# Seven-product FFN input projection: weight pieces split in an order of their own

## The chip, the cores and the metric

One core of a Trainium2 chip runs the whole program. The metric is device time in microseconds (us) of one execution; smaller is better. A profile is one execution taken by the hardware profiler.

## What is computed

One layer of a decoder trunk on 512 tokens of width 1024: a mixer with three branches, and then a gated FFN, each between two norms. The change lies in the FFN. Cut to that, the reference is

```python
h2 = rms_norm(x, g_pre_ffn) * (1 + scale2) + shift2
gt, up = jnp.split(h2 @ w_ffn_in, 2, axis=-1)       # w_ffn_in: 1024 x 5632
f = (jax.nn.silu(gt) * up) @ w_ffn_out              # w_ffn_out: 2816 x 1024
x = x + (gate2 * rms_norm(f, g_post_ffn))
```

All of it is in float32. The kernel gets this precision from matrix products on reduced operands: each operand is split into a high part (a cast, on ScalarE) and a low part (the operand less its high part, on VectorE), and a product is made of three matmuls, high by high, high by low and low by high.

## The kernel before

The hidden width of 2816 is 22 row blocks of 128. Two row blocks make a **unit**, so there are 11 units (u = 0 to 10), each with its gate and its up columns. Within a unit the product h2 by w_ffn_in is seen as a 2 x 2 block product: the weights in two row blocks by two halves of the 1024 inputs, the tokens in two halves of 256. Eight block products would be needed; the kernel forms seven (numbered 1 to 7) from sums of weight blocks and sums of token blocks. For each product q of unit u there is one **piece** of weights, 128 x 1024, and `split` (L153) makes its high part `whi` on ScalarE (L154) and its low part `wlo` on VectorE (L155). Four buffers hold the high and four the low parts, so four pieces can be alive.

What a piece is split from is said in `wino_piece` (L274). Pieces 1, 2, 4 and 7 come from the raw weights `wraw` (7 after a VectorE sum into them, L284, made when piece 4 is split). Pieces 5, 6 and 3 come from one tile `wsum` in turn: VectorE forms it for piece 5 (L282); when piece 5 is split, GpSimd issues a transfer that adds a block of raw weights into the tile, for piece 6 (L291); when piece 6 is split, another one for piece 3. For units 0 and 1 the first sums are made by transfers too (`wino_open`, L261). There are two `wsum` tiles and four raw tiles, loaded by SyncE's queue (L253).

`step` (L1159) makes one product: it fetches its piece, runs `flush()`, and issues 24 matmuls (L1171). Products 1, 2, 3 and 5 multiply token tiles in `hbh`/`hbl`; 4, 6 and 7 multiply the token sums `tx`. Two products add into a bank that another has begun: product 2 into that of 1, product 3 into that of 5. Between them the gate work is done: `gated_m1` (L1192) makes three VectorE operations, called c here, after product 7 (L1195, which reads 7; L1196, which reads the bank of product 5; L1198, which reads 4), then three ScalarE operations `sg` (L164 to L166), and leaves two VectorE products for the next `flush`. `gated_m0` (L1184) and `third_of` (L1201) do the like for the other quarters.

The order of the work in this stage is the order of the code, engine by engine: a manual schedule holds for TensorE, VectorE and ScalarE. Two things set it. The products of a unit from 2 on run in the order 5, 1, 4, 6, 7, 2, 3 (loop from L1302); units 0 and 1 run together, amid the steps of the norm that makes the last tokens' h2. And `piece()` (L226) decides when a piece is split: the list `WINO` (L239) names the pieces in the order in which they are used, and each `step` first splits, in the order of that list, up to `at["look"]` pieces ahead (4 in this stage, 3 for a while, 3 elsewhere). So the split of the piece three products on stands in the queues of ScalarE and VectorE ahead of what follows this product there.

After the last unit the second FFN product follows. Its operand `f4s[u]` is split into `fparts` by `f_split` (L1330), and its first rows also take in a modulation row made from `mod_w` on the side (`mods_in_turn`, L961, whose matmuls are `pmr`).

Of the kernel before, what the change touches and what calls it, by code (L numbers as in the profile page):

```python
# [8 lines left out]
FR = mybir.dt.float32r  # L9
# [4 lines left out]
P = 128  # L14
# [18 lines left out]
def hybrid_block(ctx: ExitStack, tc, x, c, mod_w, mod_b, g_pre_mix, g_post_mix, g_pre_ffn,  # L33
# [29 lines left out]
    hl = gp.tile([P, KD, T], FR, tag="h_lo", name="hl")  # L63


    tqs = ExitStack()
    tq = tqs.enter_context(tc.tile_pool(name="tq", bufs=1, side="right"))

    def q2(name, dt=F32):
        return tq.tile([P, 512], dt, tag="q2", name=name, bufs=12)  # L70
# [82 lines left out]
    def split(hi, lo, src):  # L153
        act.copy(hi, src)  # L154
        vec.tensor_tensor(lo, src, hi.bitcast(F32), ALU.subtract)  # L155
# [12 lines left out]


    chunks, pieces, raws = [], [], []  # L170
    at = {"dma": 0, "split": 0, "use": 0, "raw": 0, "look": LOOK}

    def w_cols(src, c0, n=256):

# [27 lines left out]
    def split_piece():  # L202
# [20 lines left out]
        pieces[at["split"]] = (hi, lo)  # L223
        at["split"] += 1

    def piece():  # L226

        i = at["use"]
        at["use"] += 1
        while at["split"] < min(i + at["look"], n_pieces):  # L230
            with tc.high_priority() if at["split"] < 5 else nullcontext():
                split_piece()
        return pieces[i]


# [1 line left out]

    NU = MF // 2
    WINO = [(u, q) for q in (1, 2, 5, 6, 7, 4, 3) for u in range(2)]  # L239
    WINO += [(u, q) for u in range(2, NU) for q in (5, 1, 4, 6, 7, 2, 3)]  # L240
    units = {}
    late_pool = {}

# [875 lines left out]
    for tp2 in range(2):  # L1119
        tbs = (2 * tp2, 2 * tp2 + 1)  # L1120
        pos = {tb: [bank("pwo") for _ in range(2)] for tb in tbs}
        ws = {}
        if tp2:
            at["look"] = 4
        for k in range(KD - LATE):
            ws[k] = piece()
            for tb in tbs:
                wo_mm(pos[tb], tb, ws[k], k)
            if todo and k >= 2:
                h2_tiles(todo.pop(0))  # L1130
# [25 lines left out]
        while later:  # L1156
            later.pop(0)()

    def step(q, o, start, stop):  # L1159

        hi, lo = piece()
        flush()
        for g in range(2):
            cs = slice(g * 256, g * 256 + 256)
            for k in range(4):
                if q in tb_of:
                    xh, xl = hbh[:, tb_of[q], k, :], hbl[:, tb_of[q], k, :]
                else:
                    xh, xl = (t_[k // 2][:, k % 2, :] for t_ in tx[q])
                for part, (a_, b_) in enumerate(((hi, xh), (hi, xl), (lo, xh))):  # L1170
                    pe.matmul(o[:, cs], a_[:, g, k, :], b_,  # L1171
                              start=(start and g + k + part == 0),
                              stop=(stop and k == 3 and part == 2), skip_group_check=True)
# [29 lines left out]
        vec.tensor_tensor(u2, p5, u2, ALU.add)  # L1203
        gated_m0(f4, u2, 1)

    def f_parts(u, parts_):
        split(parts_[0], parts_[1], f4s[u])
        fhs.append(parts_[0])
        fls.append(parts_[1])
    f4s, fhs, fls, pts = [], [], [], {}  # L1210
    rest = ctx.enter_context(ExitStack())
    rest.enter_context(tc.manual_schedule(engines={ET.PE, ET.DVE, ET.Activation}))
    if True:
        late_mm(2)
        chain_sq(2, pos[2])
        chain_norm(2, pos[2])
        late_mm(3)
        chain_x1(2, pos[2], lambda: t2("sq2"))
        chain_sq(3, pos[3])
        chain_norm2(2)  # L1220
        chain_norm(3, pos[3])
        chain_h2(2)
        ma.close()
        fp = ctx.enter_context(tc.tile_pool(name="fp", bufs=1, reuse_waits="tile"))
        fxs = ExitStack()
        fx = fxs.enter_context(tc.tile_pool(name="fx", bufs=1, reuse_waits="tile"))
        late_pool.update(fp=fp, fx=fx)
        wino_open()
        pb_ = {1: [], 5: [], 6: [], 7: [], 4: []}

        def fresh(q):
            pb_[q].append(bank(f"pf{q}"))
            step(q, pb_[q][-1], True, True)
        u2s = [temp("u2", 512, 2) for _ in range(2)]
        fresh(1)
        act.copy(u2s[0], pb_[1][0])
        chain_x1(3, pos[3], lambda: temp("sg1", 512))
        fresh(1)
        act.copy(u2s[1], pb_[1][1])
        chain_norm2(3)  # L1240
        step(2, pb_[1][0], False, True)
        pts[0] = h2_tr(2)

        t1_, b22, t2_, t3_, t4_ = (f4_tile(n) for n in ("t1r", "b22", "t2r", "t3r", "t4r"))

        def k4(t_, u):
            return t_[:, u, :].rearrange("p (k t) -> p k t", k=4)

        def tx_tiles(q):
            tx[q] = [[q2("tx", FR).rearrange("p (k t) -> p k t", k=2) for _ in range(2)]  # L1250
                     for _ in range(2)]

        def parts_of(q, t_, u):
            for k0 in (0, 2):
                ts = slice(u * P, (u + 1) * P)
                h_, l_ = (t__[k0 // 2][:, :, ts] for t__ in tx[q])
                split(h_, l_, k4(t_, u)[:, k0:k0 + 2, :])
        tks = [slice(u * P, (u + 1) * P) for u in range(2)]
        def t1_of(u):
            vec.tensor_tensor(k4(t1_, u), raws2[0, u], pts[u][0], ALU.subtract)  # L1260
            split(hbh[:, 3, :, tks[u]], hbl[:, 3, :, tks[u]], k4(t1_, u))
            act.copy(k4(b22, u), pts[u][1])
        t1_of(0)
        chain_h2(3)
        at["look"] = 3
        step(2, pb_[1][1], False, True)
        at["look"] = 4
        pts[1] = h2_tr(3)
        t1_of(1)
        tx_tiles(6)  # L1270
        for u in range(2):
            vec.scalar_tensor_tensor(k4(t2_, u), k4(t1_, u), -1.0, k4(b22, u), op0=ALU.mult,
                                     op1=ALU.subtract)
            parts_of(6, t2_, u)
        for u in range(2):
            f4s.append(f4_tile("f4"))
            gated_m0(f4s[u], pb_[1][u], 0)
            flush()
        fresh(5)
        fresh(5)  # L1280
        tx_tiles(7)
        for u in range(2):
            vec.tensor_tensor(k4(t3_, u), k4(b22, u), pts[u][0], ALU.subtract)
            parts_of(7, t3_, u)
        for u in range(2):
            fresh(6)
            vec.tensor_tensor(u2s[u], pb_[6][u], u2s[u], ALU.add)
        for u in range(2):
            vec.tensor_tensor(k4(t4_, u), raws2[1, u], k4(t2_, u), ALU.add)
        tx_tiles(4)  # L1290
        for u in range(2):
            parts_of(4, t4_, u)
            split(hbh[:, 2, :, tks[u]], hbl[:, 2, :, tks[u]], k4(b22, u))
        fresh(7)
        fresh(7)
        for u in range(2):
            fresh(4)
            gated_m1(f4s[u], pb_[4][u], pb_[5][u], pb_[7][u], u2s[u])
        for u in range(2):
            step(3, pb_[5][u], False, True)  # L1300
            third_of(f4s[u], pb_[5][u], u2s[u])
        for u in range(2, NU):  # L1302
            f4s.append(f4_tile("f4"))
            p5 = bank("pf5")
            step(5, p5, True, True)
            if u == NU - 1:
                t_ = fp.tile([P, 2, 2, T], FR, tag="raw4", name="fparts", bufs=1)
                f_parts(0, (t_[:, 0], t_[:, 1]))
            p1, u2 = bank("pf1"), temp("u2", 512, 2)
            step(1, p1, True, True)  # L1310
            act.copy(u2, p1)
            p4 = bank("pf4")
            step(4, p4, True, True)
            p6 = bank("pf6")
            step(6, p6, True, True)
            vec.tensor_tensor(u2, p6, u2, ALU.add)  # L1316
            p7 = bank("pf7")
            step(7, p7, True, True)
            gated_m1(f4s[u], p4, p5, p7, u2)
            step(2, p1, False, True)  # L1320
            gated_m0(f4s[u], p1, 0)
            step(3, p5, False, True)
            third_of(f4s[u], p5, u2)
        flush()
    at["look"] = LOOK
    fxs.close()
    tqs.close()
    fo = ctx.enter_context(tc.tile_pool(name="fo", bufs=1, reuse_waits="tile"))

    def f_split(u):  # L1330

        f_parts(u, [fo.tile([P, 2, T], FR, tag="f4o", name="fparts", bufs=10) if u < 6
                    else f4_tile("fparts", FR) for _ in range(2)])
    f_split(1)

    def mah_late():
        t_ = wp.tile([P, 1024], FR, tag="whi", name="mah")
# [7 lines left out]

    def fo_mm(o, tb, w, k0, cs):
        for k in range(2):
            mm3(o[:, cs], fhs[k0 // 2][:, k, blk(tb)], fls[k0 // 2][:, k, blk(tb)],
                w[0][:, k, cs], w[1][:, k, cs], k0 + k == 0, k0 + k == MF - 1)

    NPF = MF // 2
# [77 lines left out]
```

## Time and profile before

| what | value |
|---|---|
| runs, median (lowest to highest of 3) | 883.24 us (882.63 to 884.37) |
| the profiled execution's own time | 881.74 us |
| its span, first to last instruction | 880.0 us |
| granted TensorE clock, mean of the span | 0.958 |
| TensorE busy | 778.7 us (88%) |
| VectorE busy | 561.9 us (64%) |
| ScalarE busy | 423.1 us (48%) |
| GpSimd busy | 149.5 us (17%) |
| stage of the seven products, first to last of its matmuls | 424.4 to 741.4 us |

In profile lines, PE is TensorE, DVE VectorE, ACT ScalarE, POOL GpSimd and SP SyncE. A line of a timeline gives start and duration in us, the engine, the line of the program, the operation, "out<-in" by the program's tile names, the shape, and in brackets how long the engine had been idle before it and what released it. A granted clock of 1.0 is full speed. Busy time of TensorE counts a matmul to its modelled end, and neighbours overlap, so the distance between starts is the better measure.

### The profile page before, as it was taken

The numbers are of one execution on the slowest core, as the hardware profiler recorded it, in microseconds if no ns is written. First come the engines' busy times: TensorE is split into PE (matmuls) and PEld (weight loads), VectorE is DVE, ScalarE is ACT, GpSimd is POOL, SyncE is SP. The second block draws the span as 40 slices with busy tenths as digits, with TensorE's granted clock in tenths as the row PEclk, the third lists the DMA queues.
The fourth block names the chain that finished last, engine by engine and source line by source line (L and its number), as shares of the span: only waits on it lengthen the run. The fifth ranks groups of instructions, "written<-read, shape, count | busy, mean of one in ns | idle before, by whom it ended". The sixth has DMA issues, their size and how long they took to land. (4 is left out here: it accounts for less than half of the span.)

```text
span 880.0 us, 11357 instructions
## 1 busy us (share of the span) xinstructions
PE 778.7 (88%) x4357; PEld 670.8 (76%) x4357; DVE 561.9 (64%) x812; ACT 423.1 (48%) x707; POOL 149.5 (17%) x193
## 2 busy tenths in 40 slices
PE   4899999999999999999778777887779778889997
PEld 3779887767788888878668776887779777768886
DVE  5999776688465665469568654666555656772224
ACT  5558445757663736247455434444334445442212
POOL 4354323346201020110120101010110101000000
PEclk9999999999999999999969988988889899999999
DMA  9963422124166877485759167535664336452302
GB/s 280 291 198 96 144 70 74 48 95 146 58 206 180 263 189 253 99 304 148 188 99 239 32 137 144 110 61 118 144 129 97 80 79 180 155 171 104 108 0 96
DMA packets 122597, 123.51 MB, mean 140 GB/s; under 512 B 4076, under 2 KB 95264, under 8 KB 122544
## 3 DMA queue, kind: packets, MB, share of 16 engines
q1 hardware_dynamic: 111120, 100.67, 37.4%
q0 software_dynamic: 10656, 21.06, 13.9%
q10 hardware_dynamic: 768, 1.07, 0.3%
q8 instruction: 34, 0.56, 0.3%
q14 instruction: 19, 0.16, 0.1%
HBM read 103.38 MB, written 2.10 MB: 120 GB/s over the span
## 5 line engine op out<-in xcount | busy, mean ns | idle before, releaser
L155 DVE TENSOR_TENSOR wlo<-wraw,whi 128x1024 fp32r<-128x1024 f32 (+1 forms) x133 | 162.8, 1234 | 115.0 <-ACT whi L154 114.4
L154 ACT CAST whi<-wraw 128x1024 fp32r<-128x1024 f32 (+1 forms) x133 | 136.6, 1032 | 133.6 <-PE pgt L159 32.6
L1171 PE MATMUL pf<-hbh,whi 128*128 128x256 f32 x352 | 109.8, 312 | 62.5 <-DVE c L1196 53.2
L1171 PEld LDWEIGHTS pf<-hbh,whi 128*128 128x128 f32 x352 | 76.0, 216 | 65.3 <-issue 55.3
L1171 PE MATMUL pf<-hbl,whi 128*128 128x256 f32 x352 | 107.5, 305 | 0.1
L1171 PE MATMUL pf<-hbh,wlo 128*128 128x256 f32 x352 | 106.9, 304 | 0.0
L1171 PE MATMUL pf<-tx,whi 128*128 128x256 f32 x528 | 95.5, 282 | 2.0 <-ACT whi L154 1.0
L155 DVE TENSOR_TENSOR wlo<-wsum,whi 128x1024 fp32r<-128x1024 f32 x33 | 40.2, 1224 | 81.7 <-ACT whi L154 81.7
L1171 PEld LDWEIGHTS pf<-tx,whi 128*128 128x128 f32 x528 | 81.1, 188 | 2.6 <-ACT whi L154 1.2
L1171 PE MATMUL pf<-tx,wlo 128*128 128x256 f32 x264 | 75.3, 285 | 2.8 <-DVE wlo L155 2.7
L1171 PEld LDWEIGHTS pf<-hbl,whi 128*128 128x128 f32 x352 | 76.1, 216 | 0.5 <-DVE hbl L155 0.4
L158 PE MATMUL pgt<-hh,whi 128*128 128x512 f32 x192 | 75.7, 394 | 0.0
L1171 PEld LDWEIGHTS pf<-hbh,wlo 128*128 128x128 f32 x352 | 75.5, 215 | 0.0
L160 PE MATMUL pgt<-hh,wlo 128*128 128x512 f32 x192 | 75.4, 393 | 0.0
L159 PE MATMUL pgt<-hl,whi 128*128 128x512 f32 x192 | 75.0, 390 | 0.0
L154 ACT CAST whi<-wsum 128x1024 fp32r<-128x1024 f32 x33 | 34.2, 1041 | 78.3 <-DMA wsum<-wraw 53.5
L291 POOL DMA_DIRECT2D wsum<-wraw x22 | 26.0, 1182 | 261.1 <-DVE wlo L155 246.6
L158 PE MATMUL pfo<-whi,fparts 128*128 128x512 f32 x154 | 61.4, 399 | 2.5 <-ACT fparts L154 2.5
L160 PE MATMUL pfo<-whi,fparts 128*128 128x512 f32 x154 | 61.7, 401 | 0.5 <-DVE fparts L155 0.5
L159 PE MATMUL pfo<-wlo,fparts 128*128 128x512 f32 x154 | 61.3, 398 | 0.0
L1171 PEld LDWEIGHTS pf<-tx,wlo 128*128 128x128 f32 x264 | 49.7, 188 | 4.5 <-DVE wlo L155 4.4
L991 DVE SCALAR_TENSOR_TENSOR macc<-wraw,sc,macc 128x512 f32<-128x512 f32 x56 | 42.9, 766 | 10.0 <-ACT macc L989 5.5
(389 smaller groups left out, 1688.7 us busy)
## 6 DMA issues: line engine op xcount, KB each, us to landing
wraw<-in_w_ffn_in_dram SPq DMA_DIRECT2D x44, 512.0 KB, 6.6
wraw<-in_w_in_dram SPq DMA_DIRECT2D x20, 1024.0 KB, 5.2
wraw<-in_mod_w_dram SPq DMA_DIRECT2D x16, 1024.0 KB, 5.9
wsum<-wraw POOLq DMA_DIRECT2D x24, 512.0 KB, 6.1
wraw<-in_w_ffn_out_dram SPq DMA_DIRECT2D x10, 1024.0 KB, 5.4
wraw<-in_mod_w_dram SPq DMA_DIRECT2D x16, 512.0 KB, 6.2
wraw<-in_w_o_dram SPq DMA_DIRECT2D x8, 1024.0 KB, 5.8
gate<-gate POOLq DMA_DIRECT2D x14, 256.0 KB, 4.0
```

The source lines that it names most:

```text
L154: act.copy(hi, src)
L155: vec.tensor_tensor(lo, src, hi.bitcast(F32), ALU.subtract)
L158: pe.matmul(o, whi, xhi, start=start, stop=False)
L159: pe.matmul(o, whi, xlo, start=False, stop=False)
L160: pe.matmul(o, wlo, xhi, start=False, stop=stop)
L291: nc.gpsimd.dma_start(un["s"], un[0][q - 5], accum_op=ALU.add)
L991: vec.scalar_tensor_tensor(acc, mw[:, r], c_, acc, op0=ALU.mult, op1=ALU.add)
L1171: pe.matmul(o[:, cs], a_[:, g, k, :], b_, start=(start and g + k + part == 0), stop=(stop and k == 3 and part == 2), skip_group_check=True)
```

## The change

Five things are edited.

1. The list `WINO` no longer follows the products' order. From unit 3 on, the piece of product 3 of the unit before comes third, behind pieces 5 and 1; the last unit's own piece 3 comes last. `step` now gets the unit and looks its piece up by (unit, product), so the products keep their order.
2. The first `step` calls get a smaller look-ahead each (3, 3, 2, 1, then an explicit `split_to(wino0 + 5)`, then 2 and 3), and the output projection's second half looks 3 pieces ahead where it looked 4.
3. In units 0 and 1, the token sums of product 7 are made before the first gate products, and these stand ahead of the first product 6.
4. The hidden parts of unit 1 are split in the last unit, ahead of its product 3, where they were split after all units.
5. The hidden parts of units 1 to 3 are split in halves into tiles of the pool `tq`, which is no longer closed; the pool `fo` has 4 buffers where it had 10.

```diff
+    def split_to(n):
+        while at["split"] < min(n, n_pieces):
...
+                split_piece()
...
     WINO = [(u, q) for q in (1, 2, 5, 6, 7, 4, 3) for u in range(2)]
-    WINO += [(u, q) for u in range(2, NU) for q in (5, 1, 4, 6, 7, 2, 3)]
+
+    for u in range(2, NU):
+        WINO += [(u, 5), (u, 1)] + [(u - 1, 3)] * (u > 2) + [(u, q) for q in (4, 6, 7, 2)]
+    WINO.append((NU - 1, 3))
...
-        if tp2:
-            at["look"] = 4
...
-    def step(q, o, start, stop):
-
-        hi, lo = piece()
+    wino0 = at["use"]
+
+    def step(u, q, o, start, stop, ahead=4):
+
+        i = at["use"]
+        at["use"] += 1
+        split_to(i + ahead)
+        hi, lo = pieces[wino0 + WINO.index((u, q))]
         flush()
...
+        if u < 4:
+            for parts_ in (fhs, fls):
+                parts_.append([q2("fparts", FR) for _ in range(2)])
+            for m in range(2):
+                split(fhs[u][m], fls[u][m], f4s[u][:, m, :])
...
-        fresh(1)
+        fresh(1, 3)
         act.copy(u2s[0], pb_[1][0])
         chain_x1(3, pos[3], lambda: temp("sg1", 512))
-        fresh(1)
+        fresh(1, 3)
         act.copy(u2s[1], pb_[1][1])
         chain_norm2(3)
-        step(2, pb_[1][0], False, True)
+        step(0, 2, pb_[1][0], False, True, 2)
...
-        at["look"] = 3
-        step(2, pb_[1][1], False, True)
-        at["look"] = 4
+        step(1, 2, pb_[1][1], False, True, 1)
         pts[1] = h2_tr(3)
+        split_to(wino0 + 5)
         t1_of(1)
+        fresh(5, 2)
...
+        fresh(5, 3)
+        tx_tiles(7)
...
-            step(3, p5, False, True)
+            if last:
+                f_split(1)
+            step(u, 3, p5, False, True)
             third_of(f4s[u], p5, u2)
```

How the queues change is seen in the built programs. VectorE in a steady unit, before, from the low part of its piece 2 to the third c (`wsum_4731` is this unit's sum tile, `wsum_4970` the next unit's, `pf5` and `pf7` the banks of products 5 and 7):

```order
L155 TENSOR_TENSOR wlo_4906<-wraw_4725,whi_4905 128x1024
L155 TENSOR_TENSOR wlo_4935<-wsum_4731,whi_4934 128x1024
L1316 TENSOR_TENSOR u2_4874<-pf6_4933,u2_4874 128x512
L282 TENSOR_TENSOR wsum_4970<-wraw_4967 128x1024
L155 TENSOR_TENSOR wlo_4973<-wsum_4970,whi_4972 128x1024
L1195 TENSOR_TENSOR c2_5001<-pf7_4963,u2_4874 128x512
L1196 SCALAR_TENSOR_TENSOR c2_5001<-pf5_4841,c2_5001 128x512
L1198 TENSOR_TENSOR c2_5001<-pf4_4904,c2_5001 128x512
L155 TENSOR_TENSOR wlo_5010<-wraw_4964,whi_5009 128x1024
```

The same place now (line numbers have moved; `wsum_4701` is this unit's sum tile, `wsum_4940` the next unit's):

```order
L154 TENSOR_TENSOR wlo_4906<-wraw_4695,whi_4905 128x1024
L287 TENSOR_TENSOR wsum_4940<-wraw_4937 128x1024
L154 TENSOR_TENSOR wlo_4943<-wsum_4940,whi_4942 128x1024
L1337 TENSOR_TENSOR u2_4874<-pf6_4933,u2_4874 128x512
L154 TENSOR_TENSOR wlo_4974<-wraw_4934,whi_4973 128x1024
L1203 TENSOR_TENSOR c2_5001<-pf7_4972,u2_4874 128x512
L1204 SCALAR_TENSOR_TENSOR c2_5001<-pf5_4841,c2_5001 128x512
L1206 TENSOR_TENSOR c2_5001<-pf4_4904,c2_5001 128x512
L154 TENSOR_TENSOR wlo_5010<-wsum_4701,whi_5009 128x1024
```

Piece 3 (the row that reads this unit's sum tile) has gone from the second row to the last, behind the c's, and piece 1 of the next unit from behind the c's to ahead of them. ScalarE's casts have moved in the same way. ScalarE in units 0 and 1, before, from the first copy of product 1's bank on:

```order
L1236 COPY u2_3800<-pf1_3802 128x512
L1081 ACTIVATE sg1_3833,st_3765<-x1_3361 128x512
L1081 ACTIVATE sg1_3836,st_3765<-x1_3361 128x512
L154 CAST whi_3843<-wsum_3787 128x1024
L1239 COPY u2_3801<-pf1_3842 128x512
L150 ACTIVATE st_3765<-st_3765,eps_c_117 128x1
L151 ACTIVATE st_3765<-st_3765 128x1
L154 CAST whi_3876<-wsum_3792 128x1024
L154 CAST hbh_3359<-t1r_3915 128x4x128
L1262 COPY b22_3916<-pt2_3910 128x512
```

And now:

```order
L1257 COPY u2_3796<-pf1_3798 128x512
L1086 ACTIVATE sg1_3829,st_3761<-x1_3361 128x512
L1086 ACTIVATE sg1_3832,st_3761<-x1_3361 128x512
L153 CAST whi_3839<-wraw_3696 128x1024
L1260 COPY u2_3797<-pf1_3838 128x512
L149 ACTIVATE st_3761<-st_3761,eps_c_117 128x1
L150 ACTIVATE st_3761<-st_3761 128x1
L153 CAST hbh_3359<-t1r_3905 128x4x128
L1283 COPY b22_3906<-pt2_3900 128x512
L153 CAST whi_3950<-wsum_3783 128x1024
```

The casts of the two pieces 5, which read `wsum`, stood ahead of the second copy and ahead of the first transposed half `t1r`; the first of them now stands behind both, and a cast of raw weights stands in its place.

More of the change, by code (lines that the diff above doesn't have):

```diff
@@ L63, in hybrid_block @@
     hl = gp.tile([P, KD, T], FR, tag="h_lo", name="hl")
-    tqs = ExitStack()
-    tq = tqs.enter_context(tc.tile_pool(name="tq", bufs=1, side="right"))
+    tq = ctx.enter_context(tc.tile_pool(name="tq", bufs=1, side="right"))
     def q2(name, dt=F32):
@@ L170, in hybrid_block @@
     chunks, pieces, raws = [], [], []
-    at = {"dma": 0, "split": 0, "use": 0, "raw": 0, "look": LOOK}
+    at = {"dma": 0, "split": 0, "use": 0, "raw": 0}
     def w_cols(src, c0, n=256):
@@ L224, in split_piece @@
         at["split"] += 1
+    def split_to(n):
+        while at["split"] < min(n, n_pieces):
+            with tc.high_priority() if at["split"] < 5 else nullcontext():
+                split_piece()
     def piece():
@@ L229, in piece @@
         at["use"] += 1
-        while at["split"] < min(i + at["look"], n_pieces):
-            with tc.high_priority() if at["split"] < 5 else nullcontext():
-                split_piece()
+        split_to(i + LOOK)
         return pieces[i]
@@ L1204, in third_of, with f_parts, f_split @@
         gated_m0(f4, u2, 1)
[L1206 to L1209, printed above, removed]
+    def f_parts(u, hi, lo):
+        split(hi, lo, f4s[u])
+        fhs.append([hi[:, m, :] for m in range(2)])
+        fls.append([lo[:, m, :] for m in range(2)])
+    def f_split(u):
+        if u < 4:
[3 more added lines that the diff above has]
+                split(fhs[u][m], fls[u][m], f4s[u][:, m, :])
+        else:
+            f_parts(u, *[fo.tile([P, 2, T], FR, tag="f4o", name="fparts", bufs=4) if u < 6
+                         else f4_tile("fparts", FR) for _ in range(2)])
     f4s, fhs, fls, pts = [], [], [], {}
@@ L1229, in hybrid_block, with fresh @@
         pb_ = {1: [], 5: [], 6: [], 7: [], 4: []}
-        def fresh(q):
+        def fresh(q, ahead=4):
+            u = len(pb_[q])
             pb_[q].append(bank(f"pf{q}"))
-            step(q, pb_[q][-1], True, True)
+            step(u, q, pb_[q][-1], True, True, ahead)
         u2s = [temp("u2", 512, 2) for _ in range(2)]
-        fresh(1)
+        fresh(1, 3)
         act.copy(u2s[0], pb_[1][0])
         chain_x1(3, pos[3], lambda: temp("sg1", 512))
-        fresh(1)
+        fresh(1, 3)
         act.copy(u2s[1], pb_[1][1])
         chain_norm2(3)
-        step(2, pb_[1][0], False, True)
+        step(0, 2, pb_[1][0], False, True, 2)
         pts[0] = h2_tr(2)
@@ L1274, in hybrid_block @@
             parts_of(6, t2_, u)
+        fresh(5, 3)
+        tx_tiles(7)
+        for u in range(2):
+            vec.tensor_tensor(k4(t3_, u), k4(b22, u), pts[u][0], ALU.subtract)
+            parts_of(7, t3_, u)
         for u in range(2):
@@ L1278, in hybrid_block @@
             flush()
[L1279 to L1284, printed above, removed]
         for u in range(2):
@@ L1299, in hybrid_block @@
         for u in range(2):
-            step(3, pb_[5][u], False, True)
+            step(u, 3, pb_[5][u], False, True)
             third_of(f4s[u], pb_[5][u], u2s[u])
@@ L1303, in hybrid_block @@
             f4s.append(f4_tile("f4"))
+            last = u == NU - 1
             p5 = bank("pf5")
-            step(5, p5, True, True)
-            if u == NU - 1:
+            step(u, 5, p5, True, True)
+            if last:
                 t_ = fp.tile([P, 2, 2, T], FR, tag="raw4", name="fparts", bufs=1)
-                f_parts(0, (t_[:, 0], t_[:, 1]))
+                f_parts(0, t_[:, 0], t_[:, 1])
             p1, u2 = bank("pf1"), temp("u2", 512, 2)
-            step(1, p1, True, True)
+            step(u, 1, p1, True, True)
             act.copy(u2, p1)
             p4 = bank("pf4")
-            step(4, p4, True, True)
+            step(u, 4, p4, True, True)
             p6 = bank("pf6")
-            step(6, p6, True, True)
+            step(u, 6, p6, True, True)
             vec.tensor_tensor(u2, p6, u2, ALU.add)
             p7 = bank("pf7")
-            step(7, p7, True, True)
+            step(u, 7, p7, True, True)
             gated_m1(f4s[u], p4, p5, p7, u2)
-            step(2, p1, False, True)
+            step(u, 2, p1, False, True)
             gated_m0(f4s[u], p1, 0)
-            step(3, p5, False, True)
+            if last:
+                f_split(1)
+            step(u, 3, p5, False, True)
             third_of(f4s[u], p5, u2)
         flush()
-    at["look"] = LOOK
     fxs.close()
-    tqs.close()
     fo = ctx.enter_context(tc.tile_pool(name="fo", bufs=1, reuse_waits="tile"))
[L1330 to L1334, printed above, removed]
     def mah_late():
@@ L1347, in fo_mm @@
         for k in range(2):
-            mm3(o[:, cs], fhs[k0 // 2][:, k, blk(tb)], fls[k0 // 2][:, k, blk(tb)],
+            mm3(o[:, cs], fhs[k0 // 2][k][:, blk(tb)], fls[k0 // 2][k][:, blk(tb)],
                 w[0][:, k, cs], w[1][:, k, cs], k0 + k == 0, k0 + k == MF - 1)
```

## The prediction

> **What bounds the kernel now.** I read four views: who waited for whom on TensorE and ScalarE between 424 and 742 us, the stage the change touches; the engines' busy time stretch by stretch; then the timeline of each engine through one unit, and the DMA's rates there. The waits (engine, line, whom it waited for: total us, times, longest us):
>
> ```profile
> PE pf L1171 <- DVE c L1196: 53.2, 10, 6.5
> PE pf L1171 <- ACT u L1239: 7.5, 1, 7.5
> ```
> ```profile
> ACT whi L154 <- DMA wsum<-wraw: 53.5, 11, 6.2
> ```
>
> TensorE's idle time here is nearly all one wait, once per unit of two row blocks: product 3 adds into bank p5, which VectorE must first have read (L1196). ScalarE meanwhile loses as much waiting for accumulating transfers into wsum. Two stretches, each from one product 3 to the next (us, then busy us and count by engine, granted clock, DMA share, GB/s):
>
> ```profile
> 602.35:630.40 28.05, 22.38 (x169) 22.20 (x169) 16.57 (x21) 11.86 (x17) 1.75 (x3) 0.87 0.55 114
> ...
> 686.40:713.80 27.40, 21.67 (x168) 21.28 (x169) 16.55 (x21) 11.82 (x17) 2.35 (x3) 0.94 0.35 78
> ```
>
> No engine fills the 28 us. The clock at 0.87 means half speed for 2 x 0.13 x 28.05 = 7.3 us; at 0.94, for 3.3 us. What does last 28 us shows in the timelines of VectorE, ScalarE and GpSimd (start, duration, in brackets the idle time before):
>
> ```profile
> 586.63 1.23 DVE L155 TENSOR_TENSOR wlo<-wsum,whi 128x1024 fp32r<-128x1024 f32 x1 [2.48 <-ACT whi L154]
> ...
> 588.57 2.35 DVE L155 TENSOR_TENSOR wlo<-wraw,whi 128x1024 fp32r<-128x1024 f32 x2
> 595.50 1.23 DVE L155 TENSOR_TENSOR wlo<-wsum,whi 128x1024 fp32r<-128x1024 f32 x1 [4.58 <-ACT whi L154]
> 596.64 0.68 DVE L1316 TENSOR_TENSOR u<-pf,u 128x512 f32<-128x512 f32 x1
> 597.25 1.22 DVE L282 TENSOR_TENSOR wsum<-wraw 128x1024 f32<-128x1024 f32 x1
> 599.65 1.23 DVE L155 TENSOR_TENSOR wlo<-wsum,whi 128x1024 fp32r<-128x1024 f32 x1 [1.19 <-ACT whi L154]
> 600.79 0.68 DVE L1195 TENSOR_TENSOR c<-pf,u 128x512 f32<-128x512 f32 x1
> 601.51 0.69 DVE L1196 SCALAR_TENSOR_TENSOR c<-pf,c 128x512 f32<-128x512 f32 x1
> ...
> 605.97 1.22 DVE L155 TENSOR_TENSOR wlo<-wraw,whi 128x1024 fp32r<-128x1024 f32 x1 [3.05 <-ACT whi L154]
> ```
> ```profile
> 594.42 1.05 ACT L154 CAST whi<-wsum 128x1024 fp32r<-128x1024 f32 x1 [5.44 <-DMA wsum<-wraw]
> ...
> 604.91 1.03 ACT L154 CAST whi<-wraw 128x1024 fp32r<-128x1024 f32 x1
> ...
> 613.62 1.05 ACT L154 CAST whi<-wsum 128x1024 fp32r<-128x1024 f32 x1
> ```
> ```profile
> 588.15 1.18 POOL L291 DMA_DIRECT2D wsum<-wraw  x1 [13.83 <-DVE wlo L155]
> ```
> ```profile
> 602.35 0.55 PE L1171 MATMUL pf<-hbh,whi 128*128 128x256 f32 x1 [5.35 <-DVE c L1196]
> ```
>
> The low part of piece 6 ends at 586.63 + 1.23 = 587.86; the transfer that turns wsum into piece 3 is issued behind it and has landed at 594.4, 6.5 us later. ScalarE's cast for piece 3 stands in its queue until then, VectorE's low part behind that cast, and behind these, in order, the sum and split of the next unit's piece 5 and the three gate operations c (L1195, L1196, L1198). So product 3 of this unit waits, through VectorE's queue, for a piece 3 that itself is needed only then. The loop is transfer, cast, VectorE queue, c.
>
> **The steady units.** The change takes the split of piece 3 out from ahead of the next unit's piece 5 and puts it behind the c's, where the next unit's piece 1 stood. First the queues alone. VectorE's pair of low parts ends at 588.57 + 2.35 = 590.9. With no transfer to wait for, there follow: the sum 1.2 (to 592.1), the cast 1.05 (593.2), its low part 1.2 (594.4), L1316 0.65 (595.0), the low part of piece 1, 1.1 (596.1), c. So c starts at 596.1 where it started at 600.79: 4.7 earlier per unit. Piece 3's cast is now wanted behind the first sigmoid, 604.91 - 600.79 = 4.1 after c, so at 600.2; its transfer landed at 594.4. That cover of 5.8 hides the transfer; were it gone, each us above it would come back per unit.
>
> The period is this, first and last c of seven like units, with those ahead and behind:
>
> ```profile
> 486.05 0.69 DVE L1195 TENSOR_TENSOR c<-pf,u 128x512 f32<-128x512 f32 x1
> ...
> 516.14 0.68 DVE L1195 TENSOR_TENSOR c<-pf,u 128x512 f32<-128x512 f32 x1
> ...
> 712.26 0.68 DVE L1195 TENSOR_TENSOR c<-pf,u 128x512 f32<-128x512 f32 x1
> ...
> 736.97 0.68 DVE L1195 TENSOR_TENSOR c<-pf,u 128x512 f32<-128x512 f32 x1
> ```
>
> (712.26 - 516.14) / 7 = 28.02. The queues would allow 28.0 - 4.7 = 23.3. But now TensorE is late next:
>
> ```profile
> 528.22 0.40 PE L1171 MATMUL pf<-tx,whi 128*128 128x256 f32 x2
> ...
> 536.86 0.28 PE L1171 MATMUL pf<-hbh,whi 128*128 128x256 f32 x1
> ...
> 539.57 0.28 PE L1171 MATMUL pf<-hbh,wlo 128*128 128x256 f32 x1
> ```
>
> A product is 24 matmuls. From 536.86 to 539.57 are 23 intervals, 0.118 each, so 2.83 a product; products 4, 6, 7 take (536.86 - 528.22) / 3 = 2.88. Product 3 may use its high part at c + 4.1 + 1.0 = c + 5.2 (two matmuls), its low part at c + (605.97 + 1.22 - 600.79) = c + 6.4; the other 22 matmuls take 2.6, to c + 9.05. Then products 5, 1, 4, 6, 7 take 14.3, the last result needs 0.3 more to drain: next c at 23.7. Two loops of 23.3 and 23.7: TensorE's decides. In it TensorE still idles: product 2 is issued by about c + 2.5, so 2.7 until the cast and 1.0 until the low part.
>
> What that costs in clock is the unknown. Idle stretches of this trace, and the clock behind them:
>
> ```profile
> 738.53 0.36 PE L1171 MATMUL pf<-hbh,whi 128*128 128x256 f32 x1 [2.35 <-DVE c L1196]
> ...
> 749.73 0.50 PE L158 MATMUL pfo<-whi,fparts 128*128 128x512 f32 x1 [2.53 <-ACT fparts L154]
> ...
> 750.99 0.80 PE L160 MATMUL pfo<-whi,fparts 128*128 128x512 f32 x1 [0.53 <-DVE fparts L155]
> 751.58 0.63 PE L158 MATMUL pfo<-whi,fparts 128*128 128x512 f32 x1
> ```
> ```profile
> 782.78 0.50 PE L968 MATMUL pmr<-mah,onesr 128*128 128x512 f32 x1 [2.09 <-ACT mah L154]
> ```
> ```profile
> L158 PE MATMUL pfo<-whi,fparts 128*128 128x512 f32 x154 | 61.4, 399 | 2.5 <-ACT fparts L154 2.5
> ```
>
> 2.35 alone left full speed (0.36, against 0.55 at 602.35). 2.53 and then 0.53, with two matmuls between, was followed by a slow stretch (0.63, where this matmul's mean is 399 ns). My 2.7 and 1.0 with two matmuls between are nearest to this second case, so I take it that the clock drops in most units. A drop holds for 3.3 or 7.3 us by the two stretches above, part of it (I estimate 1.5) over idle time; the busy part loses half. Bounds are 0 and (7.3 - 1.5) / 2 = 2.9; between, (5.3 - 1.5) / 2 = 1.9, I take 1.8. Period 25.5, and 7 x (28.02 - 25.5) = 17.6 gained (bounds 7 x 1.4 = 9.9 and 7 x 4.3 = 30.2).
>
> [...]
>
> **The other parts.** *Unit 2* is the first with the new order ahead of its c. Its pair of low parts:
>
> ```profile
> 503.97 2.35 DVE L155 TENSOR_TENSOR wlo<-wraw,whi 128x1024 fp32r<-128x1024 f32 x2
> ```
> ```profile
> 441.28 1.04 ACT L154 CAST whi<-wsum 128x1024 fp32r<-128x1024 f32 x1 [6.20 <-DMA wsum<-wraw]
> ```
>
> From its end, 506.3, c took 9.8; 5.2 now: 4.6 gained (4 to 5). *The last unit* splits its own piece 3 where it did: 736.97 - 712.26 = 24.7 stays. *The first splits*: ScalarE stood 6.20 before 441.28 with the copy of p1, the norm's step and the first transposed half queued behind it; TensorE's 7.5 for that copy is the same wait. They now go ahead of the wait: st, t1r, hbl and two xm, five rows of up to 0.7 each by the like row at 600.79, some 3 on VectorE. I take 3 off unit 0's c; bounds 0 (the second unit's piece 6 now has its own transfer in the way) and 6.2 (the whole wait). The gate products and piece 7 only change places in the queue ahead of the same c: nothing, their cover being that c waits for all of them. *Looking 3 pieces ahead in the output projection's second half*: nothing, two further pieces' matmuls hide it; without that cover one cast and low part, 2.3. *Hidden parts of unit 1 split in the last unit*: the wait of 2.53 + 0.53 at 749.73 goes, but the row at 782.78 waits for the modulation row, a chain of ScalarE, VectorE and transfers that starts no earlier. TensorE arrives some 4 us earlier and waits there instead, about 6 us: no gain, and if the clock drops behind it a loss. I take 1.5 (0 to 3). The halved splits and the kept pool add no transfer.
>
> **The sum.** 3 + 4.6 + 17.6 + 0 - 1.5 = 23.7. The profiled execution took 881.74; 881.7 - 23.7 = 858.0. The median of the runs, 883.24, lies 1.5 above it: **859.5**.
>
> **Rivals.** *Clock stays full*: 7 x 4.3 = 30.1, no loss in the tail: 883.2 - 3 - 4.6 - 30.1 = 845.5. For it the row at 738.53, against it 751.58. Chance 0.2. *Collision*: the loads of a later unit start when piece 3's transfer has landed, and fill the DMA for 7 us at 290 GB/s (forty slices of 0.7 us from 594):
>
> ```profile
> GB/s 345 339 291 292 288 291 289 292 290 191 0 0 56 193 202 184 126 18 6 0 0 0 0 0 0 0 0 0 12 0 0 0 0 23 143 190 155 114 88 122
> ```
> ```profile
> DMA to landing us min/median/max: 3.2/5.4/7.9
> ```
>
> Now the transfer for piece 6 is issued at about 594.7 into these loads, no longer behind them. It is wanted 613.62 - 600.79 = 12.8 after c, so at 608.9: it may take 14.2. Waiting for all the loads and then 6.2 makes 13.4, just inside. At 17.5 the period becomes 26.6, and the time 883.2 - 3 - 4.6 - 9.9 + 1.5 = 867. Chance 0.14. *It ends slower*: the same transfer takes over 14.2 + 4.7 = 18.9 in every unit; from there the period passes 28.0. At 20.5 the eight units lose 1.6 each, 12.8; less the 3 of the start, and with 1.5 in the tail, 883.2 becomes 894.5. The longest landing, 7.9, speaks against. Chance 0.04. *No change*: piece 3 is ready no earlier relative to c, since c waits for something else, the raw tiles of the next unit; then 883 again. But those land by 601.5 and are read by the sum at 597.25 + 28.0 = 625. Chance 0.05.
>
> **Range and chances.** The forecast has 0.57 with its own range of 852 to 866. The first rival takes the low end to 846, collision and the clock's upper bound the high end to 868. A measurement of this kernel tells about 0.2%, 1.8 us. Faster 0.91, same 0.05, slower 0.04.
>
> **What would show it.** Right: ScalarE's cast for piece 3 behind the sigmoid with no transfer wait; product 3 waiting for "ACT whi" and then "DVE wlo", 2 to 3 and 1 us; c to c near 25.5 with clock near 0.9. Wrong: a clock of 1.0 and 23.7; a cast of piece 6 that waits for its transfer; product 3 still released by L1196; the row at 782.78 waiting no longer than now.

## The result, and the profile after

The changed kernel takes 859.28 us, the median of 4 runs (857.51 to 860.47), against 882.93 of 4 runs before (881.02 to 884.37): ratio 0.973, 95% interval 0.971 to 0.976. The forecast was 859.5. The profiled execution took 860.47 with a span of 858.6, where it was 881.74 and 880.0. A time alone proves no reason, so first the profile.

Who waited for whom from 416 to 720 us (waiting engine, whom it waited for: total us, times, longest):

```profile
PE pf L1179 <- ACT whi L153: 26.9, 10, 4.8
...
PE pf L1179 <- DVE wlo L154: 8.0, 13, 1.1
...
ACT whi L153 <- DMA wsum<-wraw: 6.9, 3, 2.9
...
PE pf L1179 <- DVE c L1204: 3.9, 1, 3.9
```

The wait for the second c operation, 53.2 us in 10 times before, is left once (L1204 is the old L1196). In its place TensorE waits for piece 3's cast and then for its low part. ScalarE's 53.5 us for the accumulating transfers have shrunk to 6.9. Two units, c to c (us, then busy us and count by engine, granted clock, DMA share, GB/s):

```profile
536.20:561.20 25.00, 21.82 (x170) 21.42 (x170) 16.74 (x21) 11.93 (x17) 2.36 (x2) 0.93 0.60 126
561.20:587.00 25.80, 22.92 (x170) 22.42 (x169) 16.75 (x20) 11.92 (x17) 2.36 (x2) 0.87 0.59 123
```

The clock is still granted in part: 2 x 0.07 x 25.0 = 3.5 us at half speed in the one, 2 x 0.13 x 25.8 = 6.7 in the other; in slices of 0.5 us through the second, the granted clock is 0.50 from 566.5 to 573.0 and 1.00 in the others, but for the two slices in which it changes (0.89 and 0.78). Before, it is likewise 0.50 in the slices from 601.0 to 607.0 and 1.00 from 607.5 to 627.5. The second of the two units on VectorE, ScalarE and TensorE (start, duration, in brackets the idle time before):

```profile
561.20 0.69 DVE L1203 TENSOR_TENSOR c<-pf,u 128x512 f32<-128x512 f32 x1 [0.48 <-PE pf L1179]
561.92 0.69 DVE L1204 SCALAR_TENSOR_TENSOR c<-pf,c 128x512 f32<-128x512 f32 x1
562.65 0.69 DVE L1206 TENSOR_TENSOR c<-pf,c 128x512 f32<-128x512 f32 x1
566.39 1.23 DVE L154 TENSOR_TENSOR wlo<-wsum,whi 128x1024 fp32r<-128x1024 f32 x1 [3.05 <-ACT whi L153]
...
587.04 0.69 DVE L1203 TENSOR_TENSOR c<-pf,u 128x512 f32<-128x512 f32 x1 [0.48 <-PE pf L1179]
```
```profile
563.37 0.63 ACT L163 ACTIVATE sg<-c 128x512 f32<-128x512 f32 x1 [4.05 <-DVE c L1206]
...
565.33 1.03 ACT L153 CAST whi<-wsum 128x1024 fp32r<-128x1024 f32 x1
...
574.87 1.03 ACT L153 CAST whi<-wsum 128x1024 fp32r<-128x1024 f32 x1
```
```profile
566.41 0.58 PE L1179 MATMUL pf<-hbh,whi 128*128 128x256 f32 x1 [2.42 <-ACT whi L153]
...
567.67 0.58 PE L1179 MATMUL pf<-hbh,wlo 128*128 128x256 f32 x1 [0.46 <-DVE wlo L154]
568.05 0.42 PE L1179 MATMUL pf<-hbh,whi 128*128 128x256 f32 x1
568.26 0.41 PE L1179 MATMUL pf<-hbl,whi 128*128 128x256 f32 x1
```

This is the chain that the prediction drew. The cast for piece 3 (565.33) stands behind the sigmoid without idle time, so no transfer holds it; product 3 begins 566.41 - 561.20 = 5.2 behind c, stops for the cast (2.42) and the low part (0.46), and goes on at half speed: the last two starts are 0.21 apart, where 0.118 is full speed. VectorE now waits for TensorE ahead of c (0.48), not the other way round. The cast for piece 6 (574.87) waits for no transfer either.

The c's of units 0, 1, 2, 9 and 10:

```profile
477.04 0.69 DVE L1203 TENSOR_TENSOR c<-pf,u 128x512 f32<-128x512 f32 x1
...
484.89 0.69 DVE L1203 TENSOR_TENSOR c<-pf,u 128x512 f32<-128x512 f32 x1
...
510.34 0.69 DVE L1203 TENSOR_TENSOR c<-pf,u 128x512 f32<-128x512 f32 x1
...
689.52 0.69 DVE L1203 TENSOR_TENSOR c<-pf,u 128x512 f32<-128x512 f32 x1 [0.48 <-PE pf L1179]
...
714.61 0.69 DVE L1203 TENSOR_TENSOR c<-pf,u 128x512 f32<-128x512 f32 x1
```

From them and the rows of before, by the prediction's terms (before, after, gained; us):

| stretch | before | after | gained | predicted |
|---|---|---|---|---|
| to unit 0's c | 478.20 | 477.04 | 1.2 | 3 |
| unit 2: c of unit 1 to c of unit 2 | 30.09 | 25.45 | 4.6 | 4.6 |
| seven steady periods | 196.12 | 179.18 | 16.9 | 17.6 |
| last unit | 24.71 | 25.09 | -0.4 | 0 |
| tail, last c to the end of the span | 143.03 | 143.99 | -1.0 | -1.5 |
| span | 880.0 | 858.6 | 21.4 | 23.7 |

The medians lie 23.65 apart, 2.3 more than the two spans. Each profiled execution is one of its runs: the one before lies 1.2 below its median (881.74 against 882.93), the one after 1.2 above (860.47 against 859.28). The four runs of either kernel lie within 3.4 us.

### The profile page after: what moved, and what is told of

Its sections match the earlier page's. It is cut to its first block, busy times and chain, and to the rows that moved or that the text cites. A ratio compares the mean times of both kernels' runs of the same rounds, so it can differ in the third digit from the quotient of the medians.

```text
span 858.6 us, 11385 instructions
## 1 busy us (share of the span) xinstructions
PE 783.8 (91%) x4357; PEld 674.9 (79%) x4357; DVE 563.1 (66%) x815; ACT 424.1 (49%) x710; POOL 149.7 (17%) x193
## 4 chain that ended last, share of the span: by engine, by line
PE 67%; DVE 14%; DMA 7%; ACT 7%; issue 3%; POOL 2%; DVEq 0%; ACTq 0%; SPq 0%; POOLq 0%
PE pf L1179 18%; PE pgt L157 5%; PE pgt L159 5%; PE pgt L158 5%; DVE wlo L154 3%; PE pfo L157 3%; PE pfo L159 3%; PE pfo L158 3%; ACT whi L153 2%; DMA wraw<-in_mod_w_dram 2%; DMA wsum<-wraw 2%; PE pbr L157 2%; PE pbr L159 2%; PE pbr L158 2%; PE xbc L366 2%
## 5 line engine op out<-in xcount | busy, mean ns | idle before, releaser
L1179 PEld LDWEIGHTS pf<-hbh,whi 128*128 128x128 f32 x352 | 75.8, 215 | 32.0 <-ACT whi L153 23.4
L1179 PEld LDWEIGHTS pf<-tx,whi 128*128 128x128 f32 x528 | 82.9, 192 | 5.6 <-ACT whi L153 5.6
```

The source lines that it names most:

```text
L1179: pe.matmul(o[:, cs], a_[:, g, k, :], b_, start=(start and g + k + part == 0), stop=(stop and k == 3 and part == 2), skip_group_check=True)
```

## The experiments

**Which edit carries the gain.** *The list of before in the changed kernel:*

```diff
-    for u in range(2, NU):
-        WINO += [(u, 5), (u, 1)] + [(u - 1, 3)] * (u > 2) + [(u, q) for q in (4, 6, 7, 2)]
-    WINO.append((NU - 1, 3))
+    WINO += [(u, q) for u in range(2, NU) for q in (5, 1, 4, 6, 7, 2, 3)]
```

> The changed kernel with the list of before: piece 3 is again split ahead of the next unit's piece 5; the first splits, the last unit's halves and the pools stay as changed. Theory (the whole gain is piece 3's place in the list): c to c goes back to 28.0 us in the steady units, and with unit 2's 4.6 and seven times 2.4 given back the time is 859.3 + 21.4 = 881, within 2 us. Rival (the other four edits carry part of the gain, at the start or in the tail): 870 to 876.

Measured 880.66 us against 881.26 before, ratio 0.9988 (0.9971 to 1.0005): no difference that can be told. The c's of units 2 and 9 stand

```profile
514.66 0.68 DVE L1201 TENSOR_TENSOR c<-pf,u 128x512 f32<-128x512 f32 x1
...
710.38 0.68 DVE L1201 TENSOR_TENSOR c<-pf,u 128x512 f32<-128x512 f32 x1
```

195.72 / 7 = 27.96 apart, the period of before. *The new list alone in the kernel before* (steps look their piece up by unit and product, all else as before):

> The kernel before with the new list alone (a step looks its piece up by unit and product); first splits, hidden parts and pools as before. Theory (the list is the whole gain): the 1.2 us that the first splits brought unit 0's c are missing, the tail's loss of 1.0 is not made, so 882.9 - 4.6 - 16.9 = 861, within 2 us. Rival (the first splits or the earlier halves are needed for it): 866 to 876, with a c to c above 25.6 or a tail longer than 143 us.

Measured 862.71 us (857.74 to 865.54), ratio 0.978 (0.973 to 0.983). The c's of the same units:

```profile
509.03 0.69 DVE L1200 TENSOR_TENSOR c<-pf,u 128x512 f32<-128x512 f32 x1
...
688.08 0.69 DVE L1200 TENSOR_TENSOR c<-pf,u 128x512 f32<-128x512 f32 x1 [0.48 <-PE pf L1176]
```

179.05 / 7 = 25.58. The list is the gain of the steady units, and of unit 2: from the c of unit 1 to that of unit 2 are 25.46 here, and 30.09 with the old list in the changed kernel. The other edits together make no difference that can be told in the first of these two runs, and in the second what is missing to 859.28 is within the scatter. *The hidden parts of unit 1 split late again*, still in halves:

```diff
-            if last:
-                f_split(1)
...
     fxs.close()
+    f_split(1)
```

> The changed kernel with the hidden parts of unit 1 split after all units again, as before, still in halves. Theory (the wait for these parts only moves to the modulation row's matmuls): TensorE waits about 3 us for the hidden parts at the start of the second FFN product and about as much less for the modulation row; the time stays at 859.3, within 1.5, and by my term would fall by up to 1.5. Rival (the earlier halves save the wait): 2 to 3 us slower, 861 to 863.

Measured 859.17 us, the changed kernel 859.28. TensorE's waits behind the last unit, first in the changed kernel, then in this one:

```profile
743.51 0.50 PE L973 MATMUL pmr<-mah,onesr 128*128 128x512 f32 x1 [0.97 <-ACT mah L153]
...
760.08 0.49 PE L973 MATMUL pmr<-mah,onesr 128*128 128x512 f32 x1 [4.14 <-ACT mah L153]
```
```profile
724.96 0.50 PE L157 MATMUL pfo<-whi,fparts 128*128 128x512 f32 x1 [1.12 <-ACT fparts L153]
...
725.97 0.50 PE L159 MATMUL pfo<-whi,fparts 128*128 128x512 f32 x1 [0.28 <-DVE fparts L154]
...
758.27 0.80 PE L973 MATMUL pmr<-mah,onesr 128*128 128x512 f32 x1 [4.10 <-ACT mah L153]
```

The wait for the hidden parts is 1.4 in halves, where the theory had 3 and where it was 3.1 before. Splitting them earlier turns it into 0.97 at the modulation row's first matmuls; 4.1 at its second ones, 2.09 before, stands in both. That edit is worth nothing here, as the theory had it.

**What bound the kernel before.** *Before, without the transfer for piece 3:*

```diff
-        if q in (5, 6):
+        if q == 5 or (q == 6 and u < 2):
             nc.gpsimd.dma_start(un["s"], un[0][q - 5], accum_op=ALU.add)
```

> The kernel before without the transfer that adds the second block of weights for piece 3 in units 2 to 10: piece 3 is split from the sum tile as piece 6 left it, so this part of the sum is left out. Order of all queues as before. Theory (the 28.0 us of before are the loop of transfer, cast, VectorE's queue and c): c comes 4 to 5 us earlier in each unit, c to c 23.3 to 24, TensorE's wait for L1196 falls below 2.5 and the time is 882.9 - 8 x 4.3 = about 848 us. Rival (the transfer is hidden and something else, such as the raw loads or VectorE's own work, sets c): c to c stays 27 to 28, 878 to 883.

Measured 843.68 us against 883.44, ratio 0.955 (0.953 to 0.958). The c's of units 3 and 9, and one period with the columns as above:

```profile
536.54 0.68 DVE L1195 TENSOR_TENSOR c<-pf,u 128x512 f32<-128x512 f32 x1
...
677.89 0.68 DVE L1195 TENSOR_TENSOR c<-pf,u 128x512 f32<-128x512 f32 x1
```
```profile
536.50:559.90 23.40, 20.64 (x171) 20.05 (x170) 16.51 (x21) 11.73 (x17) 1.19 (x1) 1.00 0.48 119
```

141.35 / 6 = 23.56: three periods of 23.37 at a granted clock of 1.00 and then three of 23.75. With every queue in its old order, that transfer alone was worth 28.02 - 23.56 = 4.5 us a unit, and what the queues then allow is close to the 23.3 that the prediction read off the timeline. That it was the wait, and not the transfer's traffic, follows from the run of the list alone: it keeps every transfer and still goes from 28.0 to 25.6.

**What the clock costs.** *Thirty matmuls more in each unit*, between products 2 and 3:

```diff
+            if not last:
+                for _ in range(30):
+                    pe.matmul(p6[:, 0:256], hbh[:, 0, 0, 0:128], hbh[:, 0, 0, :],
+                              start=True, stop=True, skip_group_check=True)
             step(u, 3, p5, False, True)
```

> The changed kernel with 30 matmuls of 128x128 by 128x256 more in each unit from 2 to 9, between products 2 and 3, written to the bank of product 6 that has been read by then; their results are not used. They take 30 x 0.118 = 3.5 us at full speed and fill the gap in which product 3 waits for the cast and low part of its piece. Theory (the period is 23.7 by the waits alone, and half clock behind the gap makes it 25.6): granted clock 1.0 in the steady units, c to c of 23.7 to 24.0, 859.3 - 8 x 1.7 = about 846 us. Rival (the clock costs nothing here, VectorE's queue or the DMA already sets 25.6): c to c of 25.6 or more and 859 to 866.

Measured 843.28 us, ratio 0.957 (0.954 to 0.960): with 240 matmuls more, it is 16 us faster than the changed kernel. A stretch of 30 us in it:

```profile
550.00:580.00 30.00, 30.00 (x257) 29.94 (x256) 21.83 (x26) 13.86 (x19) 3.53 (x3) 1.00 0.73 152
```

Clock 1.00, and TensorE busy throughout: 198 matmuls of 0.118 are 23.4, so the fill takes the room that the waits took. From unit 3 to unit 9, c to c is 23.4 to 23.6. *With 10 of them*, once ahead of product 3 and once behind its first two matmuls:

> The changed kernel with only 10 filling matmuls (1.2 us at full speed) ahead of product 3 in units 2 to 9, results not used. The wait for the cast shrinks from 2.4 to about 1.3 us, the 0.5 to 1.0 for the low part stays, so TensorE idles about as long as its waits allow and the loop by waits alone stays 23.7. Theory (half clock follows when the two gaps together pass some length between the 1.8 of one gap that kept full speed and the 2.9 to 3.4 that lost it): about 2 us of idling is near the lower end, so clock 1.0, c to c 23.7 and about 846 us. Rival (any stop of TensorE in this place brings half clock, whatever its length): c to c 25.6 and 859.

> The changed kernel with the 10 filling matmuls behind product 3's first two, so between the wait for the cast (which stays 2.4 us) and that for the low part, which they hide; units 2 to 9, results not used. Theory (it is the two gaps together, with almost no work between, that bring half clock; one gap of 2.4 does not): clock 1.0, c to c 23.7 to 24.0, about 846 us. Rival (the single gap of 2.4 is enough): clock 0.87 to 0.93 as in the changed kernel, c to c 25.6, 859 us.

Measured 848.95 us, ratio 0.959 (0.955 to 0.963), and 849.51, 0.961 (0.957 to 0.965). Theory and rival missed in both runs: the units are of two kinds. In the second kernel, the beginning of product 3 in three units that follow each other:

```profile
540.05 0.58 PE L1182 MATMUL pf<-hbh,whi 128*128 128x256 f32 x1 [2.43 <-ACT whi L153]
...
565.18 0.39 PE L1182 MATMUL pf<-hbh,whi 128*128 128x256 f32 x1 [2.43 <-ACT whi L153]
...
588.61 0.39 PE L1182 MATMUL pf<-hbh,whi 128*128 128x256 f32 x1 [2.42 <-ACT whi L153]
```

The same idle time, once followed by half speed (0.58) and twice not (0.39). Of its six intervals from c to c between units 3 and 9, four are 23.4 and two, each with a slow product 3, 25.1 and 25.2; in the first kernel (1.23 to 1.35 and 0.76 of idling) four are 23.4 to 23.6 and two 24.9. So 23.4 is the period without a clock loss, and one loss costs 1.5 to 1.8. The length of the gap alone does not decide. Nor is a gap of 2.4 needed: in the first kernel, gaps of 1.23 and 0.76 were followed by half speed in one unit (the matmul at 541.01 takes 0.53, the starts behind it lie 0.21 apart) and not in another (0.38 at 637.74). In the kernel before without piece 3's transfer, TensorE waits 0.8 for a cast and 0.8 for a low part in each unit, and the three periods of 23.37 kept a granted clock of 1.00; TensorE also waits 1.2 for c in four units and in the others not. What makes the periods of 23.75 longer by 0.4 was not shown.

**What is late next.** *Piece 3 ahead of piece 1:*

```diff
-        WINO += [(u, 5), (u, 1)] + [(u - 1, 3)] * (u > 2) + [(u, q) for q in (4, 6, 7, 2)]
+        WINO += [(u, 5)] + [(u - 1, 3)] * (u > 2) + [(u, q) for q in (1, 4, 6, 7, 2)]
```

> The changed kernel with piece 3 of the unit before one place earlier in the list: behind the next unit's piece 5 but ahead of its piece 1, so its cast stands ahead of the sigmoid and its low part ahead of the c's; piece 1 takes the place behind them. Theory (the period is 2.4 + 0.5 us of waiting for piece 3's parts and about 1.8 of half clock behind it): product 3 follows product 2 without a gap, the clock stays at 1.0, product 3 ends 5 us earlier and with it the cast for piece 6 and piece 3's transfer, c to c becomes 20 to 21 us (seven products of 2.85), and the time 859.3 - 8 x 5 = about 820 us. Rival (the transfer decides again, as before the change: the low part of piece 6 ends 16 us behind c, its transfer lands 6.5 later, then cast, low part and c): c to c of 25 us, the cast for piece 3 waiting for the transfer, and 850 to 860.

Measured 848.24 us, ratio 0.964 (0.960 to 0.968). The clock stays at 1.00 in the profile's steady units, as expected, with 1.8 of TensorE's waiting for c in each (16.2 us in 9 times), but c to c is 23.9, not 20 to 21. On ScalarE and VectorE:

```profile
578.80 1.05 ACT L153 CAST whi<-wsum 128x1024 fp32r<-128x1024 f32 x1 [1.25 <-DMA wsum<-wraw]
583.20 0.63 ACT L163 ACTIVATE sg<-c 128x512 f32<-128x512 f32 x1 [3.35 <-DVE c L1206]
...
585.16 1.04 ACT L153 CAST whi<-wraw 128x1024 fp32r<-128x1024 f32 x1
```
```profile
579.89 1.23 DVE L154 TENSOR_TENSOR wlo<-wsum,whi 128x1024 fp32r<-128x1024 f32 x1 [0.47 <-ACT whi L153]
581.03 0.68 DVE L1203 TENSOR_TENSOR c<-pf,u 128x512 f32<-128x512 f32 x1
...
586.23 1.22 DVE L154 TENSOR_TENSOR wlo<-wraw,whi 128x1024 fp32r<-128x1024 f32 x1 [3.06 <-ACT whi L153]
...
591.76 0.68 DVE L1211 TENSOR_TENSOR u<-pf,u 128x512 f32<-128x512 f32 x1
```

The rival came nearer than the theory. The low part of piece 6 ends 15.1 behind the c of 557.12, where the rival had 16, the transfer lands 6.6 later, the cast for piece 3 waits 1.25 for it, VectorE's low part 0.47 for the cast, and c follows at once. But this adds only some 0.5: in the one period in which VectorE does not wait there, from 653.21 to 676.55, c to c is still 23.3. What sets that is a second loop: c, three sigmoid operations, the cast behind them, its low part, and only behind that on VectorE the gate products and the last quarter's sum (L1211). VectorE idles 3.06 for a cast that stands in ScalarE's queue, and ScalarE idles 3.35 just ahead. That gave a new theory for the changed kernel, where the transfer has time to spare: write that split ahead of the sigmoid.

```diff
-    def gated(dst, g, u, sg):
...
+    def gated(dst, g, u, sg, early=False):
...
+        if early:
+            split_to(at["use"] + 4)
         sigm(sg, g)
```

First for the first gate of units 2 to 10, then for all three.

> The changed kernel, where in units 2 to 10 the split that stands behind the first sigmoid (piece 3's in units 3 on) is written between the three c's and that sigmoid: its cast goes ahead of the three sigmoid operations on ScalarE, its low part stays behind the c's on VectorE. ScalarE idles for some 4 us there, so the cast costs the sigmoid nothing. Theory (two loops: TensorE's through product 3's wait, and one of ScalarE and VectorE from c over sigmoid, cast, low part and the products behind it, which the 23.6 us of the kernel with filling matmuls shows): both lose the about 2 us that cast and low part stood behind the sigmoid. Product 3's low part comes at c + 3.4 where it came at c + 6.4, the gap falls to under 1 us, the clock stays 1.0, c to c 21.4 to 21.9, and the time 859.3 - 8 x 3.9 = about 828 us. Rival (piece 3's transfer decides: low part of piece 6 at c + 13, 6.5 to 7.2 us of transfer, and the cast wanted at c + 21): c to c above 23 with the cast waiting for the transfer, 840 to 850.

> As in the kernel with the split ahead of the first sigmoid, and the same for the other two gates of units 2 to 10: the splits of pieces 4 and 6 of the next unit go ahead of their sigmoids. Theory (the loop of ScalarE and VectorE is what remains above TensorE's seven products): the casts no longer stand behind two shorter sigmoids of 1.3 us each, the loop falls below TensorE's 7 x 2.85 = 20.0, c to c becomes 20.0 to 20.7, and the time 859.3 - 8 x 5.3 = about 817 us. Rival (the transfers decide: piece 6's is issued behind piece 5's low part and now wanted 2 us earlier): no gain over the first of the two, c to c 21.5 to 23 and casts waiting for transfers, 828 or more.

Measured 827.37 us, ratio 0.938 (0.935 to 0.940), and 816.15 us, 0.924 (0.922 to 0.927). In the first, product 3 waits once, for the low part, and c to c is 21.3:

```profile
551.87 0.68 DVE L1205 TENSOR_TENSOR c<-pf,u 128x512 f32<-128x512 f32 x1
...
573.15 0.68 DVE L1205 TENSOR_TENSOR c<-pf,u 128x512 f32<-128x512 f32 x1
```
```profile
555.19 0.38 PE L1179 MATMUL pf<-hbh,wlo 128*128 128x256 f32 x1 [1.17 <-DVE wlo L154]
```

In the second, two c's that follow each other and the stretch between:

```profile
552.70 0.69 DVE L1205 TENSOR_TENSOR c<-pf,u 128x512 f32<-128x512 f32 x1 [0.48 <-PE pf L1179]
...
573.11 0.69 DVE L1205 TENSOR_TENSOR c<-pf,u 128x512 f32<-128x512 f32 x1 [0.47 <-PE pf L1179]
```
```profile
552.70:573.10 20.40, 20.09 (x170) 19.89 (x169) 16.75 (x20) 12.04 (x18) 2.36 (x2) 1.00 0.72 155
```

20.4 us of which TensorE is busy 20.1, at full clock: its seven products are now the bound, and this version is 43 us faster than the changed kernel.

## Why the prediction was right, point by point

**The loop through the transfer** was the bound of before: without the transfer 23.56, with it 28.0, and the list alone, which keeps the transfer, 25.58.

**The sum** by its terms missed by 2.3: 21.4 us of span were gained where 23.7 were forecast, 1.8 of it at unit 0's c. That the median came out at 859.28 for a forecast of 859.5 is in part luck, since the two profiled executions lie 1.2 below and 1.2 above their medians.

**The steady units** were right in the sum, 25.60 against 25.5, from two terms that were each a little off and cancel. The period without clock loss was put at 23.7; the units that kept full clock show 23.4. The clock loss was put at 1.8 a unit; it is 25.6 - 23.4 = 2.2 by these, and 16.0 / 8 = 2.0 by the kernel with thirty matmuls more. The gaps were put at 2.7 and 1.0; they are 2.42 and 0.46 to 0.76, the second shortest in the unit shown, where the two matmuls ahead of it already run slowly. That the clock drops "in most units" was too mild: it drops in each of the seven.

**The reason for the drop** was only half right. The prediction took two gaps with two matmuls between as the case that drops, a single 2.35 as one that does not. The single 2.43 does both. Gaps of 2.42 and 0.46 to 0.76, together 2.9 to 3.2, lost clock in each steady unit, by spells of about 3.5 or 6.7 us (the 2 x 0.07 x 25.0 and 2 x 0.13 x 25.8 above); of the 6.7 in the unit shown, 0.46 stood over idle time, where the prediction estimated 1.5. A safe length of a gap does not follow from these runs: with ten matmuls ahead of product 3, 1.23 and 0.76, together 2.0, lost it in one unit and kept it in another. What decides was not shown, and stays open.

**Unit 2** gained 4.6 as worked out. **The last unit** lost 0.4 where nothing was forecast. It is not the clock that holds c there: in the kernel with piece 3 ahead of piece 1, this stretch (676.55 to 701.27) took 24.7, and the granted clock was 1.00 from 670 to 700 us. The list leaves the last unit's own piece 3 ahead of its c's, and the old wait is still there, on ScalarE and then, for the cast, on VectorE (2.57). Where the 0.4 come from is open. The cast in the changed kernel:

```profile
710.50 1.05 ACT L153 CAST whi<-wsum 128x1024 fp32r<-128x1024 f32 x1 [2.90 <-DMA wsum<-wraw]
```

**The first splits** gave 1.2 at unit 0's c where 3 was forecast. The first matmul of the stage, before and in the changed kernel:

```profile
424.41 0.28 PE L1171 MATMUL pf<-hbh,whi 128*128 128x256 f32 x1
```
```profile
427.20 0.28 PE L1179 MATMUL pf<-hbh,whi 128*128 128x256 f32 x1
```

From there unit 0's c came after 53.8 and now after 49.8: 4.0 gained, while the stage itself began 2.8 later. Over the profiles of this study that stretch is 52.7 to 54.5 in the three kernels with the old first splits and 49.5 to 51.6 in the nine with the new ones, while the stage's start lies anywhere from 423.1 to 427.2. TensorE's 7.5 us of waiting for the copy of product 1's bank are gone (0.3 is left), but waits of 4.2 for a piece's cast and 3.6 for the cast of a transposed half stand in their place. So there is a gain inside the stage, of 2 to 4 us: 2.2 and 2.8 between the kernels that have the same list, 4.0 between before and changed. It can't be divided between the look-ahead and product 7's earlier token sums, which all nine kernels have together, and whether the later start is scatter or theirs is not settled.

**The tail** was right in its mechanism (the wait moves to the modulation row: 0.97 and 4.14, together 5.1 where 6 was forecast, and as much as the 2.53, 0.53 and 2.09 of before). Its price of 1.5 can't be told from nothing: 859.17 against 859.28.

**The rivals.** *Clock stays full* did not come, but its 845.5 is near the 843.28 of the kernel whose thirty matmuls keep the clock; the two with ten, which lose it in two of six periods, take 849. *Collision* did not decide. All transfers into the sum tile, from issue to landing:

```profile
DMA to landing us min/median/max: 3.1/6.1/9.3
```

The longest is 9.3 where the prediction allowed 14.2, and the cast for piece 6 waited for none in the steady units.

## What to carry to other kernels

When a wait is taken out of a queue, look at what stands in its old place and what the moved work now stands behind: here a cast went from behind a transfer to behind a sigmoid, and a place one step further ahead, in idle time of the same engine, was worth another 32 us, more than the change's 24. Work the period out for each loop by itself (transfer, the queues of the two smaller engines, TensorE's products); removing the largest gains only down to the next. And price an idle gap of TensorE with the clock behind it: here gaps of 2.9 to 3.2 us a unit cost about 2 more in slow matmuls.

## What the runs showed of the hardware that was not expected

Filling a gap with 3.5 us of useless matmuls made each unit 2 us shorter (25.6 to 23.5). A granted clock of 0.50 here spaces matmuls of 256 columns 0.21 apart, not twice 0.118. And a gap of 2.43 us lost the clock in some units and not in others of one execution, in the same place of the program (0.58 and 0.39 for the matmul behind it); in another kernel 1.23 and 0.76 did the same (0.53 and 0.38).
